# A hybrid S5 and sparse-attention encoder layer: transposing all of x ahead of the modulation, narrower value products, and other shares of stream work

## The chip, the cores and the metric

The kernel runs on one core of one Trainium2 chip. A core has a matrix engine (PE, with its weight loads shown as PEld), a vector engine (DVE), a scalar engine (ACT), a general engine (POOL) and a sync engine (SP) that here mostly issues DMA transfers. The engines run their own instruction queues in order and wait for each other through semaphores. The metric is the device time of one execution in microseconds (us); lower is better.

## What is computed

One layer over 1024 prompt tokens and 32 sample tokens, all treated together as 1056 columns. Cut to what matters here:

```python
mod = silu(c) @ w_mod + b_mod                  # w_mod is 1024 x 3072
shift, scale, gate = split(mod, 3)
h = rms_norm(x, g_norm) * (1 + scale) + shift
z = h @ w_in                                   # u | zs | q | k | v | za | qi | ki | wi | gm
ys = S5 state space model over u, GELU, GLU, SiLU gate zs
score = sum_h wi * relu(qi . ki);  keep the top k keys per query
o = softmax(q . k over kept keys) @ v          # 8 heads of 64, prompt in chunks of 64 (causal)
merged = sigmoid(g_s) * (ys @ w_ps) + sigmoid(g_a) * ((o * silu(za)) @ w_pa)
x_new = x + gate * (merged @ w_o);  y = rms_norm(x_new, g_final)
```

Prompt and sample rows have different c, so different scale and shift. All is float32. The kernel gets its precision by splitting a factor into a high part (fp32r) and a low part, and by three products: high x high, high x low, low x high (`mm3`).

## The kernel before

**Groups of tokens.** The 1056 tokens are cut in three groups of 256, 384 and 416 columns (`BW`, lines 19 and 20; 32 of the last 416 are the sample). Group g has row tiles of 128 tokens (`ROWS`, line 60). h is kept transposed, features on the partitions, in eight slices k of 128 features: `hH` and `hL`, one pair of tiles for each group.

**START.** The order of the beginning is written out by hand in the string `START` (line 48). All engines follow it in program order (a manual schedule is open until line 793). Its tokens, with their digits:
- `sq i`, `ss i`, `sc i`: row tile i of x is squared and summed on ACT (`xsquare`), its reciprocal root made on DVE and POOL (`xrstd`), and scaled on DVE (`xscale`).
- `mm`, `row`, `co`, `ap`: a piece of w_mod is multiplied with the condition vectors on PE (`mod_mm`, L286), copied by ACT (`mod_row`, L291), turned into columns on PE (`mod_cols`, L296), and made into scale and shift by three DVE operations (`mod_apply`). Before, a piece (j, h) is 256 columns of the scale (h = 0) or shift (h = 1) part, loaded in one transfer of 1 MB.
- `xt g k`: PE transposes slice k of group g into PSUM (`xtrans`, L231). `hf g k`: ACT reads that PSUM, applies scale and shift (`xmod`, L237 and L239). `sp g k`: DVE splits the result into hH and hL (`xsplit`, by `split`, L77 and L78).
- `ub q n k`: the three products of slice k of group n with the weights of output block q (0 or 1) of the S5 input u (`ublock`, L271 to L273). `ue`: ACT copies the finished block out.
- `wl q`: the u weights are split. `a n`: n of the small DVE operations that prepare the S5 constants (the list `todo`) are issued. `ld..`: further loads are issued.

Loads are issued by SP in the order of lines 749 to 759 and of the `ld` tokens: three row tiles of x, two pieces of w_mod, the u weights, two more pieces, the second u weights, three more row tiles, and so on, so that x and w_mod arrive mixed. Row tiles lie in borrowed buffers; groups are transposed when their slice of the modulation is known.

**Stream.** The other weight products are jobs of the class `Stream` (`Z`). A job multiplies 128 output features with all three groups: 8 slices x 3 groups x 3 products. `Z.run(us)` issues some microseconds' worth of stream steps on PE at that place of the program, `Z.until(name)` issues steps until a job is done, `Z.upto(name)` says how far the stream may go. So each later stage has PE work between its own steps.

**After START.** `ssm_consts` (line 525) makes S5 constants: four transposes on PE (L529), two copies on ACT, one more transpose (L533), a copy on DVE. Then the loop of line 790 empties `todo` on DVE and asks 2.0 us of stream for each 2.0 us of it. The S5 stage, the glu jobs (their operands ygH and ygL are split on ACT and DVE from the gelu result), the indexer (L1230) and the choice of the keys (L1573, L1575) follow.

**Attention.** Heads are worked in pairs p = 0 to 3. For a pair the loop of line 1720 goes through items: a block of 128 queries (`Rows`), or the sample. For each: scores on PE (L1409), maxima on DVE (L1415), exponentials on ACT (L1422), normalizing, transposes of the probabilities on PE (L1502) and their split into PH and PL (`turn`, L1504 and L1505), and for every second block the value products (`out`, L1519 and L1521) over two blocks of queries, 256 columns, and all their key tiles. The last key tile of such a pair of blocks is not admitted for the first block; `turn` clears its first 128 columns on POOL (L1507, L1508). Each step of the loop asks the stream for `f = FA[p][e] + FF * (i + 1)` us. Pair 3 has the jobs m0 to m7 (products with w_ps) to ask for; behind the loop `Z.until("m7")` issues the rest, and then the products with w_pa begin, first those with the attention result b3 of pair 3.

Of the kernel before, what the change touches and what calls it, by code (L numbers as in the profile page):

```python
# [30 lines left out]
WB = 5  # L31
# [9 lines left out]
KA, LA = 5.0, 1.0  # L41
RE = 2.9
LAG, RS, MS, RM, RB = 4.5, 4.6, 0.008, 14.0, 1
FA, FF, SA, SB = ((1.4, 1.3), (1.45, 1.45), (1.35, 1.35), (1.4, 1.4)), 0.08, 1.0, 2.5
# [19 lines left out]
def body(nc, tc, I, O, dbg=None):  # L64
# [129 lines left out]
    XG, XW = {}, []  # L194

    def xload(i):
        g, r, n = ROWS[i]
        if i < 2:
            xt = stg.tile([128, D], F32, name="xt", tag="stg")
        elif i < 5:  # L200
            xt = XH[i // 4][:, D * (i == 3):D * (i == 3) + D]
        elif i == 5:
            xt = pa.tile([128, D], F32, name="xt", bufs=1)
        else:
            if i % 2 == 0:
# [21 lines left out]
    def xtrans(g, k):  # L227
        px = ps_z("px")
        PX[g, k] = px
        for r, n in enumerate(GROW[g]):  # L230
            te.transpose(px[:, r * 128:r * 128 + n], XG[g][r][:n, k * 128:(k + 1) * 128], idf[:n, :n])  # L231

    def xmod(g, k):
        px = PX.pop((g, k))
        hf = HX[g, k] = pa.tile([128, GM], F32, name="hf", bufs=HF)[:, :BW[g]]
        np_ = min(BW[g], T - B0[g])
        se.activation(hf[:, :np_], px[:, :np_], AF.Identity, bias=sh[:, k, 0:1], scale=scl[:, k, 0:1])  # L237
# [501 lines left out]
    def load(x):  # L739
# [6 lines left out]
        for f in xl:  # L746
            f()
# [1217 lines left out]
```

## Time and profile before

| what | value |
|---|---|
| runs, median of 3 | 998.66 us (997.09 to 1001.67) |
| profiled execution, its time | 997.35 us |
| profiled execution, its span from first to last instruction | 995.6 us |
| mean granted PE clock | 0.991 of full speed |
| DMA in the span | 124.24 MB, mean 125 GB/s |

The profile is of one execution. Its page gives the busy time of each engine and, in 40 slices of the span, the busy share in tenths. Other views of the same trace give stretches of the span (busy us of each engine and the number of its instructions, then the granted clock, the DMA share, GB/s), or a timeline (start in us, duration in us, engine, line, operation, output <- inputs, shapes, how often; in brackets the idle time of the engine before it and what ended that). Durations of matmuls are modelled and overlap; the distance of two starts is what one costs PE. The slices of the other engines and of DMA are:

```profile
DVE  4669979995686868979998977767678786895543
ACT  3642244433555655867999356665676565443211
```

### The profile page before, as it was taken

The numbers are of one execution on the slowest core, as the hardware profiler recorded it, in microseconds if no ns is written. First come the engines' busy times: TensorE is split into PE (matmuls) and PEld (weight loads), VectorE is DVE, ScalarE is ACT, GpSimd is POOL, SyncE is SP. The second block draws the span as 40 slices with busy tenths as digits, with TensorE's granted clock in tenths as the row PEclk, the third lists the DMA queues.
The fourth block names the chain that finished last, engine by engine and source line by source line (L and its number), as shares of the span: only waits on it lengthen the run. The fifth ranks groups of instructions, "written<-read, shape, count | busy, mean of one in ns | idle before, by whom it ended". The sixth has DMA issues, their size and how long they took to land.

```text
span 995.6 us, 16923 instructions
## 1 busy us (share of the span) xinstructions
PE 962.1 (97%) x6034; PEld 898.8 (90%) x6034; DVE 758.3 (76%) x1748; ACT 526.7 (53%) x1127; POOL 229.2 (23%) x435
## 2 busy tenths in 40 slices
PE   4999999999999999999999999999999999999997
PEld 2789999999899899999999999999899988998786
DVE  4669979995686868979998977767678786895543
ACT  3642244433555655867999356665676565443211
POOL 2202400000000003333322852333323222430000
PEclk8899999999999999999999999999999999999999
DMA  9923424536585221424213440231349302662311
GB/s 312 300 66 104 131 70 129 123 94 168 193 255 154 93 64 43 136 80 136 90 65 98 148 145 22 87 120 32 97 132 337 106 23 93 197 211 94 117 64 63
DMA packets 134255, 124.24 MB, mean 125 GB/s; under 512 B 20256, under 2 KB 114932, under 8 KB 134172
## 3 DMA queue, kind: packets, MB, share of 16 engines
q1 hardware_dynamic: 133232, 122.62, 40.0%
q8 instruction: 47, 0.77, 0.3%
q10 hardware_dynamic: 780, 0.52, 0.2%
q14 instruction: 36, 0.29, 0.1%
q0 software_dynamic: 160, 0.03, 0.0%
HBM read 87.74 MB, written 34.83 MB: 123 GB/s over the span
## 4 chain that ended last, share of the span: by engine, by line
PE 54%; DVE 11%; ACT 10%; issue 4%; DMA 1%; POOL 1%; SPq 0%; POOLq 0%; ACTq 0%; DVEq 0%
PE pz L271 9%; PE pz L272 8%; PE pz L273 8%; ACT junkb L1573 7%; PE pss L1409 3%; PE pt L1502 3%; DVE junk L1575 3%; PE psm L1936 3%; PE psm L1934 3%; PE psm L1935 3%; PE pspo L1521 2%; PE pspo L1519 2%; PE pss L1230 2%; PE pss L1231 2%; PE psm L271 1%
## 5 line engine op out<-in xcount | busy, mean ns | idle before, releaser
L271 PE MATMUL pz<-hH,wh 128*128 128x384 f32 (+4 forms) x760 | 258.2, 340 | 0.8 <-ACT zf L1323 0.8
L272 PE MATMUL pz<-hL,wh 128*128 128x384 f32 (+4 forms) x760 | 249.9, 329 | 0.0
L273 PE MATMUL pz<-hH,wl 128*128 128x384 f32 (+4 forms) x760 | 249.8, 329 | 0.0
L264 POOL TENSOR_TENSOR wl<-raw,wh 128x256 fp32r<-128x256 f32 (+1 forms) x176 | 126.4, 747 | 123.6 <-ACT wh L259 119.5
L271 PEld LDWEIGHTS pz<-hH,wh 128*128 128x128 f32 (+1 forms) x760 | 142.5, 188 | 5.9 <-issue 1.7
L272 PEld LDWEIGHTS pz<-hL,wh 128*128 128x128 f32 (+1 forms) x760 | 141.9, 187 | 2.0
L273 PEld LDWEIGHTS pz<-hH,wl 128*128 128x128 f32 (+1 forms) x760 | 141.6, 186 | 1.3
L1573 ACT ACTIVATE junkb<-sco,thr 128x768 bf16<-128x768 f32 (+3 forms) x128 | 96.7, 756 | 29.1 <-DVE thr L1655 18.6
L1575 DVE TENSOR_SCALAR_CACHE_REDUCE junk<-sco,thr 128x1024 bf16<-128x1024 f32 (+2 forms) x96 | 105.4, 1098 | 2.2
L271 PE MATMUL pss<-hH,wh 128*128 128x256 f32 (+2 forms) x288 | 92.8, 322 | 1.5 <-ACT tg L713 1.4
L272 PE MATMUL pss<-hL,wh 128*128 128x256 f32 (+2 forms) x288 | 90.9, 316 | 0.0
L273 PE MATMUL pss<-hH,wl 128*128 128x256 f32 (+2 forms) x288 | 90.6, 315 | 0.0
L263 POOL CAST wh<-raw 128x256 fp32r<-128x256 f32 x84 | 41.2, 529 | 178.3 <-PE pz L272 163.2
L1504 ACT CAST PH<-pt 128x512 fp32r<-128x512 f32 (+2 forms) x96 | 43.0, 482 | 35.2 <-PE pt L1502 32.8
L1505 DVE TENSOR_TENSOR PL<-pt,PH 128x512 fp32r<-128x512 f32 (+2 forms) x96 | 50.4, 552 | 13.1 <-ACT PH L1504 11.9
L1238 DVE SCALAR_TENSOR_TENSOR sco<-rl,wi,sco 128x384 f32<-128x384 f32 (+6 forms) x49 | 45.6, 939 | 18.3 <-ACT rl L1233 17.5
L271 PEld LDWEIGHTS pss<-hH,wh 128*128 128x128 f32 x288 | 55.5, 193 | 3.8 <-POOL wh L263 1.6
L1233 ACT ACTIVATE rl<-pss 128x384 f32<-128x384 f32 (+6 forms) x56 | 41.1, 738 | 28.5 <-PE pss L1231 21.7
L272 PEld LDWEIGHTS pss<-hL,wh 128*128 128x128 f32 x288 | 55.3, 192 | 0.3 <-DVE hL L78 0.2
L273 PEld LDWEIGHTS pss<-hH,wl 128*128 128x128 f32 x288 | 55.2, 192 | 0.0
L1422 ACT ACTIVATE Sm<-Sm,mx 128x128 f32<-128x128 f32 (+8 forms) x68 | 52.7, 774 | 1.3 <-DVE mx L1415 1.3
L1936 PE MATMUL psm<-o,mL 128*128 128x512 f32 (+1 forms) x136 | 52.0, 382 | 0.0
(409 smaller groups left out, 2165.4 us busy)
## 6 DMA issues: line engine op xcount, KB each, us to landing
raw<-in_w_in SPq DMA_DIRECT2D x44, 512.0 KB
thD<-tg SPq DMA_DIRECT2D x16, 528.0 KB
wm<-in_w_mod SPq DMA_DIRECT2D x8, 1024.0 KB
m<-thD SPq DMA_DIRECT2D x8, 528.0 KB
tgl<-thD SPq DMA_DIRECT2D x8, 528.0 KB
rraw<-in_w_mod SPq DMA_DIRECT2D x4, 1024.0 KB
kd<-kd SPq DMA_DIRECT2D x32, 128.0 KB
xo<-in_x_prompt SPq DMA_DIRECT2D x8, 512.0 KB
```

Source lines behind the costliest of these rows:

```text
L263: ge.tensor_copy(wh[:, c], raw[:, c])
L264: leng.tensor_sub(wl[:, c], raw[:, c], f32(wh[:, c]))
L271: te.matmul(ps, wh, xh, start=first, stop=False)
L272: te.matmul(ps, wh, xl, start=False, stop=False)
L273: te.matmul(ps, wl, xh, start=False, stop=last)
L1238: ve.scalar_tensor_tensor(sco[i][:m, :nk], rl[:m, :nk], w, sco[i][:m, :nk], op0=ALU.mult, op1=ALU.add)
L1422: se.activation(P, P, AF.Exp, scale=-1.0, bias=self.mx, accum_out=self.rs)
L1504: se.copy(PH[:, b0:b1_, oc], src)
L1505: ve.tensor_sub(PL[:, b0:b1_, oc], src, f32(PH[:, b0:b1_, oc]))
L1573: se.activation(junkb[:m, :nk], x[:m], AF.Sign, bias=t, accum_out=cnt[:m, k:k + 1])
L1575: ve.tensor_scalar(junk[:m, :nk], x[:m], t, None, op0=ALU.is_lt, op1=ALU.add, accum_out=cnt[:m, k:k + 1])
L1936: te.matmul(ps, ml, wh, start=False, stop=last)
```

## The change

It has four parts.

1. **START.** All nine row tiles of x are loaded first, into the space that hH will take, then half of the u weights (256 columns, four slices), then w_mod in three pieces that hold scale and shift together (256, 256 and 512 features, `MW`), each in parts of 1 MB, and the second half of the u weights before the third piece. Each group of x is transposed as soon as its rows are scaled, two or four slices in one PSUM tile, and copied out of PSUM into tiles `XT` by ACT (`xe`) or DVE (`xd`). When a piece of the modulation is known, its slices are worked for all three groups, one slice after the other. `w n` issues n products that nobody reads. The u products of group 2 get two single PSUM banks. There are 17 of the small DVE operations in START, where there were 36.
2. **ssm_consts** asks 2.0 us of stream between its two sets of transposes.
3. **Value products.** For the last key tile only columns 128 to 255 are multiplied; the clears on POOL go.
4. **Constants.** `FA` asks 0.05 us more for each step in pairs 0 (second head) to 2, and 0.25 less in pair 3; `KA`, the delay between a load of keys and its split, is 4.2 in place of 5.0.

```diff
-WB = 5
+WB = 4
-KA, LA = 5.0, 1.0
+KA, LA = 4.2, 1.0
-FA, FF, SA, SB = ((1.4, 1.3), (1.45, 1.45), (1.35, 1.35), (1.4, 1.4)), 0.08, 1.0, 2.5
+FA, FF, SA, SB = ((1.4, 1.35), (1.5, 1.5), (1.4, 1.4), (1.15, 1.15)), 0.08, 1.0, 2.5
 START = """
-    sq0 ss0 sq1 sc0 ss1 sq2 sc1 ss2 sc2 mm00 srow ldw21 a13 xt00 row00 xt01 co00 mm01 ldw30 row01 wl00 co01
...
+    sq0 ss0 sq1 ss1 sc0 sq2 ss2 sc1 srow xt00 xt04 xd00 sq3 ss3 sc2 xd04 sq4 ss4 sc3 sq5 ss5 sc4 xt10 xt12 xd10
+    sq6 ss6 sc5 xd12 xt14 sq7 ss7 sc6 xt16 xd14 sq8 ss8 sc7 xe16 sc8 xt20 xe20 xt22 xd22 wl00 xt24 xe24 xt26 xd26 wl10
+    mm00 a10 w6 mm01 row0 w3 co0 ap0 w6 hf00 sp00 hf10 sp10 hf20 sp20 ub000 ub100 hf01 sp01 ub010 ub110 hf11 sp11
+    hf21 sp21 ub020 ub120 mm10 a2 ub001 ub101 mm11 row1 ub011 ub111 co1 ap1 ub021 hf02 sp02 hf12 sp12 ub121 hf22 sp22
+    ub002 ub102 hf03 sp03 a1 mm20 ub012 ub112 hf13 sp13 a1 ub022 ub122 mm21 hf23 sp23 ub003 ub103 mm22 wl01 ub013 ub113
+    wl11 mm23 row2 ub023 ldz co2 ap2 hf04 sp04 ub123 hf14 sp14 hf24 sp24 a1 ub004 ub104 hf05 sp05 ub014 ub114 hf15 sp15
...
     def xtrans(g, k):
-        px = ps_z("px")
-        PX[g, k] = px
-        for r, n in enumerate(GROW[g]):
-            te.transpose(px[:, r * 128:r * 128 + n], XG[g][r][:n, k * 128:(k + 1) * 128], idf[:n, :n])
+        px = PX[g, k] = ps_s("px").rearrange("p (j c) -> p j c", j=2 if g else 4)
+        for j in range(px.shape[1]):
+            for r, n in enumerate(GROW[g]):
+                te.transpose(px[:, j, r * 128:r * 128 + n], XG[g][r][:n, (k + j) * 128:(k + j + 1) * 128], idf[:n, :n])
+
+    def xkeep(g, k, copy):
+        px = PX.pop((g, k))
+        for j in range(px.shape[1]):
+            copy(XT[g][k + j], px[:, j, 0:BW[g]])
...
+    def mod_mm(m, i):
+        w = MW[m][1]
+        nk = 1024 // w
+        for k in range(nk):
+            for c in range(2):
+                o = 32 * (2 * (k % 2) + c)
+                te.matmul(pmrow[o:o + 32, 0:w], scP[:, nk * i + k], WM[m, i][:, k, c], start=nk * i + k < 2,
+                          stop=nk * i + k >= 6)
...
     def ssm_consts():
...
             se.mul(dst.rearrange("p k m -> p (k m)"), pt[:, 0:256], sgn_)
+        Z.run(2.0)
...
     def warm(n):
+        if not UP:
+            UP[-1] = ps_z("pw")
         for _ in range(n):
-            te.matmul(pmod[:, 384:512], idf, idf, start=True, stop=True)
+            te.matmul(UP[-1][:, 0:128], idf, idf, start=True, stop=True)
...
+    for i in range(9):
         xload(i)
     uload(0)
+    for m in range(3):
+        if m == 2:
+            uload(1)
+        for i in range(4 if m == 2 else 2):
+            mod_load(m, i)
...
-                if ii == 0:
-                    ge.memset(f32(PH[:, i + 1, oc]), 0.0)
-                    ge.memset(f32(PL[:, i + 1, oc]), 0.0)
...
-                for k in range(nkt):
-                    te.matmul(po[:, 0:256], X.V2[e][:, k], PH[:, k], start=k == 0, stop=False)
-                for k in range(nkt):
-                    te.matmul(po[:, 0:256], X.V2[e][:, k], PL[:, k], start=False, stop=k == nkt - 1)
+                order = [*range(nkt - 2), nkt - 1, nkt - 2]
+                for h, P in ((0, PH), (1, PL)):
+                    for k in order if h or nkt > 2 else order[::-1]:
+                        c0 = 128 * (k == nkt - 1)
+                        te.matmul(po[:, c0:256], X.V2[e][:, k], P[:, k, c0:256], start=not h and k == 0,
+                                  stop=h == 1 and k == nkt - 2)
```

More of the change, by code (lines that the diff above doesn't have):

```diff
@@ L273, in mm3 @@
         te.matmul(ps, wl, xh, start=False, stop=last)
-    sel2 = pa.tile([128, 2], F32, name="sel2", bufs=1)
+    sel4 = pa.tile([128, 4], F32, name="sel4", bufs=1)
     WM, MR_ = {}, {}
-    def mod_load(j, h):
-        wm = WM[j, h] = pa.tile([128, 8, 256], F32, name="wm", tag="wm", bufs=WB)
-        c = (1024, 0)[h] + 256 * j
-        sp.dma_start(wm, w_mod[:, c:c + 256].rearrange("(k p) e -> p k e", p=128))
-    def mod_mm(j, h):
-        for k in range(8):
-            te.matmul(pmrow[32 * (k % 4):32 * (k % 4) + 32, 256 * h:256 * h + 256], scP[:, k], WM[j, h][:, k],
-                      start=k < 4, stop=k >= 4)
@@ L289, in mod_row @@
-    def mod_row(j, h):
-        MR_[j, h] = pa.tile([128, 256], F32, name="mrow", bufs=2)
-        se.copy(MR_[j, h], pmrow[:, 256 * h:256 * h + 256])
-    def mod_cols(j, h):
-        for i in range(2):
-            ch = (8, 0)[h] + 2 * j + i
-            te.matmul(pmod[:, 2 * ch:2 * ch + 2], MR_[j, h][:, 128 * i:128 * i + 128], sel2, start=True, stop=True)
-    def mod_apply(j):
-        kk = slice(2 * j, 2 * j + 2)
-        ks = slice(8 + 2 * j, 10 + 2 * j)
-        bc2 = lambda ap: ap.unsqueeze(2).to_broadcast([128, 2, 2])
-        ve.tensor_tensor(scl[:, kk], pm[:, ks], bc2(bmod[:, ks]), op=ALU.add)
+    MW = ((0, 256), (256, 256), (512, 512))
@@ new lines, in mod_row, with mod_cols, mod_apply @@
+    def mod_row(m):
+        w = MW[m][1]
+        MR_[m] = pa.tile([128, 512], F32, name="mrow", bufs=1)[:, 0:w]
+        se.copy(MR_[m], pmrow[:, 0:w])
+    def mod_cols(m):
+        c0, w = MW[m]
+        for i in range(w // 128):
+            k = c0 // 128 + i
+            te.matmul(pmod[:, 4 * k:4 * k + 4], MR_[m][:, 128 * i:128 * i + 128], sel4, start=True, stop=True)
+    def mod_apply(m):
+        c0, w = MW[m]
+        k0, nk = c0 // 128, w // 128
+        kk = slice(k0, k0 + nk)
+        ks = slice(8 + k0, 8 + k0 + nk)
+        bc2 = lambda ap: ap.unsqueeze(2).to_broadcast([128, nk, 2])
+        ve.tensor_tensor(scl[:, kk], pm[:, kk, 1], bc2(bmod[:, ks]), op=ALU.add)
@@ L724, in body, with uload, uparts @@
     raw = {}
-    def uload(q):
-        raw[q] = wload(w_in[:, C_U + 128 * q:C_U + 128 * q + 128], KT, 128)
-    def uparts(q):
-        UW[q] = wparts(raw[q], KT, 128, leng=ve) if q == 0 else wparts(raw[q], KT, 128, pool=pa, heng=ge, bufs=1)
+    def uload(h):
+        if not h:
+            raw[0] = pa.tile([128, KT, 256], F32, name="uraw", bufs=1)
+        sp.dma_start(raw[0][:, 4 * h:4 * h + 4],
+                     w_in[512 * h:512 * h + 512, C_U:C_U + 256].rearrange("(k p) e -> p k e", p=128))
+    def uparts(q, h):
+        if not h:
+            UW[q] = [(pa if q else wst).tile([128, KT, 128], F32R, name=n, tag=n, bufs=2 - q) for n in ("wh", "wl")]
+        c = slice(4 * h, 4 * h + 4)
+        split(UW[q][0][:, c], UW[q][1][:, c], raw[0][:, c, 128 * q:128 * q + 128], se, ve)
     def srows():
```

103 lines of the change are left out of this document (42 added, 61 removed).

## The prediction

> **What bounds the kernel now.** I read the page first (engine shares, the span in slices), then stretches of the first 50 us with every engine beside the granted clock, then the timelines where PE is not full.
>
> ```profile
> PE 962.1 (97%) x6034; PEld 898.8 (90%) x6034; DVE 758.3 (76%) x1748; ACT 526.7 (53%) x1127; POOL 229.2 (23%) x435
> PE   4999999999999999999999999999999999999997
> ...
> 10.00:20.00 10.00, 6.39 (x57) 4.00 (x61) 6.15 (x24) 2.25 (x4) 1.15 (x2) 0.91 1.11 338
> 20.00:30.00 10.00, 9.90 (x57) 6.70 (x46) 5.27 (x21) 4.83 (x10) 5.06 (x10) 0.50 1.08 359
> 30.00:40.00 10.00, 8.62 (x84) 5.99 (x84) 5.77 (x21) 4.59 (x10) 1.40 (x2) 0.91 1.09 356
> 40.00:50.00 10.00, 10.00 (x83) 9.09 (x82) 7.20 (x22) 8.39 (x16) 0.22 (x2) 1.00 1.00 204
> ```
>
> PE bounds all but the beginning: one slice of 40 is below 9 before the last. A saving counts only if it removes PE work or PE waiting; moving stream work (the weight products that fill gaps) alone changes nothing. The stretches (busy us of PE, PEld, DVE, ACT, POOL, then clock, DMA share, GB/s) show the exception: until about 45 us the DMA engines are full at some 350 GB/s, and from 20 to 30 us PE is busy at half clock.
>
> **START, the part that can gain most.** It ends in before when PE leaves the last u product:
>
> ```profile
> 69.52 0.60 PE L529 MATMUL pt<-idf,cld 128*128 128x128 f32 x4
> 71.10 0.24 PE L533 MATMUL pt<-idf,dl 32*128 32x32 f32 x1 [0.98 <-ACT CR L530]
> 82.81 0.28 PE L271 MATMUL pz<-hH,wh 128*128 128x256 f32 x1
> 94.37 0.28 PE L271 MATMUL pz<-hH,wh 128*128 128x256 f32 x1
> 38.06 1.07 PE L286 MATMUL pmrow<-wm,scP 128*32 128x256 f32 x16
> 22.90 1.94 PE L286 MATMUL pmrow<-wm,scP 128*32 128x256 f32 x16
> 33.34 0.61 PE L296 MATMUL pmod<-sel,mrow 128*128 128x2 f32 x4 [0.50 <-ACT mrow L291]
> 36.97 0.16 DVE L302 TENSOR_TENSOR scl<-pmod,pcol 128x4 f32<-128x4 f32 x1 [3.17 <-PE pmod L296]
> 39.59 0.56 ACT L237 ACTIVATE hf<-px,sh,scl 128x256 f32<-128x256 f32 x1
> ```
>
> The end is at 69.5. One stream job, with the same 72 matmuls as 24 u blocks, takes 94.37 - 82.81 = 11.56 us at full clock, so the 48 u blocks cost 23.1. A 1 MB tile of w_mod costs PE 1.07 at full clock, 1.94 at half; a transpose costs 0.11 (row below), so 0.21 at half. The row copy and its handover stop PE for 0.50; the co products are 0.61 for four records.
>
> After the change nothing can be multiplied before all nine row tiles are squared, scaled, transposed and copied out. What sets that time is DVE, which runs in written order:
>
> ```profile
> 5.22 1.06 ACT L214 ACTIVATE sq<-xt 128x1024 bf16<-128x1024 f32 x1 [1.24 <-DMA xt<-in_x_prompt]
> 6.62 1.06 ACT L214 ACTIVATE sq<-xt 128x1024 bf16<-128x1024 f32 x1 [0.25 <-DMA xt<-in_x_prompt]
> 7.31 0.75 DVE L223 TENSOR_SCALAR xt<-xt,rstd 128x1024 f32<-128x1024 f32 x1 [0.75 <-POOL rstd L219]
> 7.97 0.15 DVE L218 TENSOR_SCALAR ss<-ss 128x1 f32<-128x1 f32 x1
> 8.04 0.20 DVE L167 COPY pcol<-pt 128x48 f32<-128x48 f32 x1
> 246.33 0.28 DVE L1041 COPY sto<-pt 64x128 f32<-64x128 f32 x1 [6.12 <-PE pt L1039]
> 56.10 0.48 ACT L561 COPY uP<-pss 128x384 f32<-128x384 f32 x1 [0.43 <-PE pss L273]
> ```
>
> Row tiles land 1.4 apart (two squares that waited for DMA), so the ninth lands near 16 and is squared by 17. DVE scales a tile in 0.66 (start to next start) and adds 0.15 for ss. Copies out of PSUM grow from 0.20 at 48 columns to 0.28 at 128, 1 ns a column: about 0.36, 0.49 and 0.52 in a run for 256, 384 and 416 columns; DVE has 8, 6 and 4 of these new ones, ACT six of 0.5. Nine scalings (5.9), nine ss (1.4), the first 14 copies (5.8) and srow (0.2) are 13.3. The first scaling, now behind two squares, starts at 7.8: without a wait the last row is scaled at 21; with the waits for transposes that DVE stands behind in its order, at 22.5. Then group 2 goes through two PSUM buffers: 32 transposes and the copies that free the buffers, 3.8 at full clock and about 7 at half. PE reaches mm00 at 26.3 (24.3 without DVE's waits, 30 at half clock). Its data is there: x, half of u and one tile are 5.9 MB, at 0.35 MB a us from 3 us on landed by 20. The start is no longer bound by DMA, but by DVE's copies, which before did not exist (ACT read PSUM directly).
>
> From mm00 to the first u block runs a chain: two tiles 2.1, six warm products between them 1.3 (twelve records, 0.106 each as a transpose), row 0.5, co 0.6, ap 0.7 (three of 0.16 and handovers), hf 0.56 and the split's first half 0.35, together 6.1. From there PE is dense: 48 blocks 23.1, six more tiles 6.4, twelve co records 1.8, and two waits that blocks only partly cover, 0.6 before slice 2 and 1.1 before slice 4. That is 33.0. DVE's splits keep up:
>
> ```profile
> 58.38 0.37 DVE L77 CAST hH<-hf 128x416 fp32r<-128x416 f32 x1
> 58.78 0.59 DVE L78 TENSOR_TENSOR hL<-hf,hH 128x416 fp32r<-128x416 f32 x1
> 59.29 0.37 DVE L77 CAST hH<-hf 128x416 fp32r<-128x416 f32 x1
> ```
>
> 0.92 for the widest group, some 2.5 for three, against 2.9 of PE per slice. The last w_mod tiles reuse buffers freed after mm10 and mm11, near 37 and 39, and so land near 42 and 45; PE wants them at 47 and later. START would end at 26.3 + 6.1 + 33.0 = 65.4; at 69.1 if PE reaches mm00 at 30, a little more if the first products are slow too (69.5); at 63.4 without DVE's waits. I take 66.5, nearer to full clock: **-3.0** (bounds -6.1 and 0, if the clock is back by the first block).
>
> The 2.0 us of stream placed between the two consts transposes covers the 0.98 of PE idle shown above: **-1.0**.
>
> **A debt that START leaves.** It runs 17 of DVE's small constant operations, where it ran 36: 19 of 0.2 are 3.8 us of DVE later, and the loop that empties them asks 3.8 more of stream. With the 2.0 above, 5.8 us of filler is missing later, where the glu jobs wait for the gelu result:
>
> ```profile
> 234.55 0.39 PE L970 MATMUL pss<-HS,G 128*128 128x133 f32 x2
> 250.29 4.38 ACT L75 CAST ygH<-yg 128x1024 fp32r<-128x1024 f32 x4
> 265.22 2.18 DVE L78 TENSOR_TENSOR ygL<-yg,ygH 128x1024 fp32r<-128x1024 f32 x2 [0.99 <-ACT ygH L75]
> 266.38 0.28 PE L271 MATMUL pz<-ygH,wh 128*128 128x256 f32 x1
> ```
>
> PE has 31.7 of other work from 234.7 to 266.4; 25.9 would be left. The chain needs 15.6 to the loaded yg, 8.8 of casts (4.38 for two of four) and 2.2 for the last subtraction, 26.6: **+0.8** (0, if the casts interleave better, to +4, if ACT's evacuations stand in between).
>
> **Half-width value products.** 4 pairs x 2 heads x 4 blocks x 2 parts = 64 matmuls go from 256 to 128 columns.
>
> ```profile
> 648.45 1.19 PE L1519 MATMUL pspo<-PH,V 128*128 128x256 f32 x8
> 649.48 1.10 PE L1521 MATMUL pspo<-PL,V 128*128 128x256 f32 x8
> 645.79 1.09 PE L1502 MATMUL pt<-idf,Sm 128*128 128x128 f32 x8
> 646.64 0.37 PE L1409 MATMUL pss<-kH,qz 128*128 128x256 f32 x1
> 644.38 0.22 PE L1409 MATMUL pss<-kH,qz 128*128 128x128 f32 x1
> 644.43 0.27 PE L1409 MATMUL pss<-kL,qz 128*128 128x128 f32 x1
> 644.55 0.40 PE L271 MATMUL pz<-hH,wh 128*128 128x416 f32 x1
> ```
>
> Eight of 256 columns take 1.03, 0.129 each. Eight transposes of 128 columns, a new weight load each, take 0.85, 0.106: half the columns are not half the time, because the load is then the limit. Two 128-column products between longer ones take 0.17, 0.085 each. So one saves 0.023 to 0.044, or up to 0.07 if its load is always early: 1.5 to 4.5 for 64. The half product stands before a full one, as the last pair of rows does, with loads less far ahead; I take 0.034: **-2.2**. The 64 clears on POOL that go hid behind PE; nothing for them.
>
> **Stream shares, KA.** Pair 3 runs some 20 steps and asks 0.25 less in each, 5.0 us; pairs 0 to 2 ask 0.05 more in 9 to 17, 2.1. So 2.9 of m7 moves behind the loop, where PE waits today:
>
> ```profile
> 841.75 0.35 PE L273 MATMUL pz<-b,wl 128*128 128x416 f32 x1
> 843.26 0.75 PE L271 MATMUL psm<-b3H,wh 128*128 128x256 f32 x3 [1.15 <-ACT b3H L75]
> 766.00:842.00 76.00, 74.60 (x507) 70.04 (x505) 57.72 (x165) 43.33 (x99) 17.78 (x45) 1.00 0.24 72
> ```
>
> It can cover 1.15, if ACT's cast of b3 isn't itself queued behind a weight cast that waits for m7: **-0.8** (0 to -1.8, with two shorter gaps behind it). In pair 3 PE idles 1.4 of 76 and DVE is busy 76%; with 7% less filler the softmax chain of DVE and ACT shows more often: **+0.8** (0 to +4). KA moves a load by under a microsecond inside that: nothing.
>
> **Sum.** -3.0 - 1.0 + 0.8 - 2.2 - 0.8 + 0.8 = -5.4 on the profiled execution's 997.35 (its span 995.6 and 1.8 around it): 991.95. The median of the three runs shown is 1.3 above the profiled one, so 993.3.
>
> **Rivals.**
> *Slow clock to mm00.* PE was granted 0.50 from 20 to 30 us although it was busy 9.90 of 10, and the new beginning is transposes with pauses between them. Then START ends at 69.5, as today, and -2.4 is left: 996.3. For it: that row. Against it: the 0.91 before and after, and the warm products. The Trainium skill ("TensorE: Matmul & The Clock Gate", Part 4: PE-mode transpose) says that transposes do not count as a busy PE in the way products do; by that this rival holds. The row agrees in part only: the half clock also lay over u products.
> *Slow clock in the slices, the slower case.* If the half clock holds for some 14 us from the first block on (it held from before 20 to past 30 here), blocks at 11.56 / 24 = 0.48 become 0.87, and each such us loses 0.45: 6.1. START ends near 75.6, the whole is +3.7: 1002.4. It decides against the change from 5.4 us of half clock on, and two such stretches give 1008. Against it: PE is then dense, and the clock was 1.00 from 40 on.
> *Pair 3 starves.* The softmax chain keeps its period and the 5.0 less stays idle: +4 in place of +0.8, and START as forecast: 996.5.
> *Everything hides.* START ends at 63.4, value products save 0.07, no debt, the end -1.8: -6.1 - 1.0 - 4.5 - 1.8 + 0.8 = -12.6: 986.1.
>
> **How the numbers follow.** My forecast 0.37, slow clock to mm00 0.22, slow slices 0.11, pair 3 starving 0.10, everything hiding 0.20. About 5 us, 0.5%, is what a measurement can tell here. The forecast lies on that edge, with two thirds of its chance beyond it (0.25), the last rival wholly (0.20), of the others 0.05: faster 0.50. Slower by over 0.5% is the slow slices that last longer than one stretch or meet another loss: 0.09. The range goes from 985 to 1001: it leaves out the slow slices and little else.
>
> **What would show it.** The start of L529 in the consts: near 66.5, and mm00 near 26 to 27; DVE full from 8 to 25 us; the granted clock from 20 to 40 us; no gap of 0.98 before L533; the gap at the first glu product; mean spacing of value products; the gap before the first b3 product, and PE's idle time in pair 3. I am wrong if DVE's copies are much faster or slower than 1 ns a column, or the clock is half behind 30 us.

## The result, and the profile after

The changed kernel takes 1011.07 us (median of 4 runs, 1007.25 to 1013.32) against 998.01 for the kernel before: ratio 1.012, 95% interval 1.0078 to 1.0162. It is slower, by some 13 us, or 1.2%; the forecast was 993.3 in a range of 985 to 1001. The profiled run of the changed kernel took 1007.25 with a span of 1005.5, so between the two profiles 9.9 us are to be explained.

The page of the changed kernel, the lines that stood first in the prediction:

```profile
PE 965.6 (96%) x6016; PEld 899.2 (89%) x6016; DVE 763.8 (76%) x1765; ACT 528.8 (53%) x1131; POOL 210.2 (21%) x363
PE   4999999999899999999999999999999999999997
```

PE is busy 3.5 us longer although it has less to compute, and the span grew by 9.9: some matmuls ran more slowly, and PE waited more. Walking through both traces by the same landmarks (PE's idle time added up between them) gives the places:

| stretch | before | after | difference | forecast |
|---|---|---|---|---|
| end of START (first S5 constants transpose) | 69.5 | 75.6 | +6.1 | -3.0 |
| PE idle in the constants | 1.0 | 0.4 | -0.6 | -1.0 |
| PE idle in the S5 stage | 1.9 | 3.4 | +1.5 | 0 |
| PE idle at the first qi0 product | 0 | 3.3 | +3.3 | +0.8 (placed at the first glu product) |
| PE idle from glu to the pairs | 3.3 | 2.3 | -1.0 | 0 |
| PE idle in the pairs | 3.7 | 4.8 | +1.1 | +0.8 |
| PE idle behind the last value product | 1.9 | 1.2 | -0.7 | -0.8 |
| 320 value products, start to next start | 40.7 | 40.4 | -0.3 | -2.2 |

They add up to +9.4 of the 9.9. Two places hold nearly all of it: START, and the stretch from the S5 stage to qi0.

**START.** Stretches of the changed kernel (busy us of PE, PEld, DVE, ACT, POOL, then granted clock, DMA share, GB/s), then PE's timeline and DVE's:

```profile
20.00:30.00 10.00, 7.38 (x33) 4.84 (x31) 5.93 (x13) 2.29 (x5) 4.35 (x5) 0.67 1.04 332
30.00:40.00 10.00, 10.00 (x77) 6.70 (x76) 4.93 (x19) 2.08 (x5) 0.15 (x2) 0.74 0.34 111
...
18.10:21.50 3.40, 3.40 (x16) 2.99 (x16) 2.40 (x6) 0.00 (x0) 0.99 (x1) 0.50 1.09 348
21.50:25.00 3.50, 1.82 (x11) 0.98 (x9) 3.06 (x8) 0.86 (x2) 2.43 (x3) 0.99 1.09 348
25.00:28.40 3.40, 2.46 (x10) 1.61 (x11) 0.88 (x1) 1.04 (x3) 0.93 (x2) 0.50 1.09 349
28.40:31.80 3.40, 3.40 (x13) 2.21 (x14) 1.69 (x3) 0.54 (x2) 0.00 (x0) 0.50 0.37 118
31.80:35.20 3.40, 3.40 (x24) 1.70 (x23) 1.40 (x3) 1.28 (x3) 0.15 (x2) 0.50 0.02 5
35.20:38.60 3.40, 3.40 (x38) 2.49 (x34) 1.94 (x11) 0.37 (x1) 0.00 (x0) 1.00 0.55 154
```

```profile
10.51 3.62 PE L223 MATMUL pss<-idf,xr 128*128 128x128 f32 x16
...
18.02 3.72 PE L223 MATMUL pss<-idf,xr 128*128 128x128 f32 x16 [0.87 <-DVE xr L215]
...
25.94 0.31 PE L223 MATMUL pss<-idf,xt 32*128 32x32 f32 x1 [1.41 <-DVE xt L215]
...
33.69 1.78 PE L291 MATMUL pmrow<-wm,scP 128*32 128x256 f32 x16
...
40.80 0.36 PE L268 MATMUL pss<-hH,wh 128*128 128x256 f32 x1
...
75.58 0.60 PE L538 MATMUL pt<-idf,cld 128*128 128x128 f32 x4
```

```profile
19.11 1.02 DVE L228 COPY xT<-pss 128x384 f32<-128x384 f32 x2 [1.15 <-PE pss L223]
23.41 0.73 DVE L215 TENSOR_SCALAR xr<-xr,rstd 128x1024 f32<-128x1024 f32 x1
24.58 1.30 DVE L215 TENSOR_SCALAR xt<-xt,rstd 32x1024 f32<-32x1024 f32 x1 [0.44 <-POOL rstd L211]
```

The first product with w_mod starts at 33.7, not at 26.3. DVE scales the last row (the 32 sample rows, whose tile lies in a staging buffer) only at 24.6 to 25.9, 3.4 later than reckoned, after standing at copies that waited for PE (1.15 in the first row) and because the sample rows take 1.30 where a full tile takes 0.73. Then the 32 transposes of group 2 take 7.75 (25.94 to 33.69) in place of 3.8: the clock is at half until 35.2. From there to the first u block it is 7.1 (forecast 6.1), and from there to the end 34.8 (33.0).

The 1.30 isn't the price of 32 partitions. In each of the 18 traces exactly one scaling takes 1.30, and it is the one that starts some 0.1 behind a clear of 0.83 on POOL. In the kernel before that scaling is a full tile of 128 partitions (first two rows; the 32 sample rows take 0.74 there), in the changed kernel the clear meets the sample rows (third row):

```profile
10.31 0.83 POOL L537 MEMSET zrow<- 16x896 f32 x1
10.40 1.30 DVE L223 TENSOR_SCALAR xh<-xh,rstd 128x1024 f32<-128x1024 f32 x1 [0.66 <-POOL rstd L219]
...
24.50 0.83 POOL L547 MEMSET zrow<- 16x896 f32 x1
```

No run moved the clear, so that it holds the scaling up is likely and not shown.

The clock column needs a caution. Its record begins with the first change of the clock, at 14.7 here, and counts as whole what lies before. The distances of the transposes tell more: the sixteen from 10.51 on take 3.62, like the sixteen from 18.02 on that ran at 0.50, so PE was at half until 14.7 too. In all 18 traces equal matmuls are 0.21 us apart ahead of the first record, where they are 0.11 apart at whole clock.

**From the S5 stage to qi0.** ACT's and then PE's timeline in the changed kernel:

```profile
259.23 0.37 ACT L1084 COPY zki<-pz 72x256 f32<-72x256 f32 x1 [3.90 <-DMA out_sim_p<-sto]
264.20 4.28 ACT L73 CAST ygH<-yg 128x1024 fp32r<-128x1024 f32 x4 [4.60 <-DMA yg<-yD]
268.38 0.48 ACT L1084 COPY zki<-pz 72x384 f32<-72x384 f32 x1
```

```profile
268.91 0.45 PE L268 MATMUL pz<-hH,wh 128*128 128x384 f32 x1 [3.27 <-ACT zki L1084]
```

ACT's second copy of the ki job stands in the written order behind casts of the gelu result, and these wait for a transfer that landed at 264.2. PE had finished its part of ki at 265.6 and waits for the PSUM buffer of that copy. In the kernel before, the same casts started at 250.29, early enough. The S5 stage is thus 14.0 late (last gelu operation on DVE 252.96 against 238.94), the stream jobs only 7.8 (first ki product 253.88 against 246.05). Counting the stream products on PE between the end of START and the first S5 product gives 381 before and 417 after: 36 more at 0.16 us are 5.8 us of filler spent early. That is the 3.8 of DVE's small operations and the 2.0 of the consts: with the new START alone the stream stands 24 products ahead, with the consts line alone 12.

### The profile page after: what moved, and what is told of

It is laid out like the page before. It is cut to its first block, busy times and chain, and to the rows that moved or that the text cites. A ratio compares the mean times of both kernels' runs of the same rounds, so it can differ in the third digit from the quotient of the medians.

```text
span 1005.5 us, 16804 instructions
## 1 busy us (share of the span) xinstructions
PE 965.6 (96%) x6016; PEld 899.2 (89%) x6016; DVE 763.8 (76%) x1765; ACT 528.8 (53%) x1131; POOL 210.2 (21%) x363
## 4 chain that ended last, share of the span: by engine, by line
PE 64%; DVE 16%; ACT 12%; issue 4%; DMA 3%; POOL 0%; SPq 0%; POOLq 0%; ACTq 0%; DVEq 0%
PE pz L268 10%; PE pz L270 10%; PE pz L269 10%; ACT junkb L1583 7%; PE pspo L1530 3%; PE pss L1420 3%; PE pt L1513 3%; DVE junk L1585 3%; PE psm L1946 3%; PE psm L1944 3%; PE psm L1945 3%; PE pss L1241 2%; PE pss L1242 2%; PE psm L268 1%; PE psm L269 1%
## 5 line engine op out<-in xcount | busy, mean ns | idle before, releaser
L261 POOL TENSOR_TENSOR wl<-raw,wh 128x256 fp32r<-128x256 f32 (+1 forms) x172 | 117.1, 710 | 139.3 <-ACT wh L256 136.7
L268 PE MATMUL pss<-hH,wh 128*128 128x256 f32 (+1 forms) x272 | 85.1, 313 | 1.8 <-DVE hH L75 1.2
L269 PE MATMUL pss<-hL,wh 128*128 128x256 f32 (+1 forms) x272 | 84.4, 310 | 0.2
L270 PE MATMUL pss<-hH,wl 128*128 128x256 f32 (+1 forms) x272 | 83.9, 309 | 0.0
L268 PEld LDWEIGHTS pss<-hH,wh 128*128 128x128 f32 x272 | 51.5, 189 | 6.5 <-DVE hH L75 1.9
L269 PEld LDWEIGHTS pss<-hL,wh 128*128 128x128 f32 x272 | 51.0, 188 | 0.9 <-DVE hL L76 0.8
L1944 PE MATMUL psm<-o,mH 128*128 128x512 f32 (+1 forms) x136 | 51.7, 381 | 0.0
```

The source lines that it names most:

```text
L261: leng.tensor_sub(wl[:, c], raw[:, c], f32(wh[:, c]))
L268: te.matmul(ps, wh, xh, start=first, stop=False)
L269: te.matmul(ps, wh, xl, start=False, stop=False)
L270: te.matmul(ps, wl, xh, start=False, stop=last)
L1944: te.matmul(ps, mh, wh, start=first, stop=False)
```

## Experiments

All ratios are against the kernel before, timed beside each kernel on the same chip.

### Which part loses: START alone, and the rest alone

The first kernel has the new START and everything else as before, the second the old START and everything else new:

```diff
 # START alone: taken back from the change
-KA, LA = 4.2, 1.0
+KA, LA = 5.0, 1.0
-FA, FF, SA, SB = ((1.4, 1.35), (1.5, 1.5), (1.4, 1.4), (1.15, 1.15)), 0.08, 1.0, 2.5
+FA, FF, SA, SB = ((1.4, 1.3), (1.45, 1.45), (1.35, 1.35), (1.4, 1.4)), 0.08, 1.0, 2.5
-        Z.run(2.0)
 # and the value products of full width, with the clears on POOL
```

> Only the new START; value products, the shares of pair 3, the key delay and the extra 2.0 us of stream are as before. Theory A (the whole loss comes from START: its own end 6.1 us later, and 3.3 us more at the glu hand-over because the S5 stage trails the stream): the first S5 constants transpose starts at 75.6, the gap of 0.98 in the consts is back, the wait of the first qi0 product is 1 to 3.5 us (2.0 us less filler was used up), total 1006 to 1012. Rival B (the other parts lose as much as START): 1001 to 1004.

> The old START with the three other parts: half-width value products, 2.0 us of stream in the consts, the new shares and the key delay. Theory A: START ends at 69.5 as before, consts gap gone (-1.0), value products -0.3 (a half product takes 60 ns where a full one took 120, but the full one behind it takes 171), tail and pair 3 cancel: 996 to 998 against 998. Rival B: these parts lose, 1000 to 1004. My blind terms would give -3.2: 995.

START alone: 1013.11, ratio 1.0145 (1.0124 to 1.0167). The rest alone: 1001.72, 1.0037 (1.0021 to 1.0052). START holds the loss, as theory A has it (a little over its range), but the rest isn't neutral: 3.4 us are lost there too, which is rival B's number for that kernel. In its trace START ends at 69.3 as before, but the first glu product comes 3.4 late (269.8 against 266.4). The two losses, 14.8 and 3.4, add up to more than the 13.1 of the whole change, so the parts act on each other. The other signs of theory A came for START alone: it ends at 75.4, the gap in the consts is back (1.00) and PE waits 1.40 at qi0. But its trace also has half-clock stretches behind waits at 243.3 and 765.6, which the profile of the changed kernel doesn't have.

### The 2.0 us of stream in the consts

Which of the parts is it? One kernel has this line alone, one has it and gives the 2.0 us back ahead of the S5 stage:

```diff
 # both
+        Z.run(2.0)
 # the second besides
-FS = (17, 2.5, 1, 1, 2.5, 7, 2.5, 0.6)
+FS = (15, 2.5, 1, 1, 2.5, 7, 2.5, 0.6)
```

> The kernel before with only the 2.0 us of stream put between the two sets of transposes of the consts. My blind term: the gap of 0.98 goes, 997.4. Theory F (2.0 us less stream is left for the S5 stage and every weight split of a stream job falls elsewhere among DVE's S5 steps; the last S5 products then wait 2 to 4 us, and a half-clock stretch of 3.4 us follows that wait): 1000 to 1002, with S5's last product near 240 in place of 234.7.

> The kernel before with the 2.0 us of stream in the consts, and 2.0 us less asked before the first block of the S5 stage (15 in place of 17), so that from there on the stream stands where it stood. Theory F (the 2.0 us cost 3.9 because a weight split of the stream then falls on DVE ahead of an S5 step while ACT has not yet cast its high part): S5 ends near 234, no wait at the last S5 products, the gap of 0.98 stays covered: 997.4. Rival I (the loss comes from the consts themselves or from the shorter debt to glu): 1000 to 1002 again.

Alone: 1002.36, ratio 1.0038 (1.0023 to 1.0054). Given back: 997.35, 0.9993 (0.9983 to 1.0003). So one line that covers a wait of 0.98 costs 3.9 us, and moving the same amount of stream back undoes all of it. Theory F holds. How it works is seen in the S5 stage, first on DVE in the kernel before:

```profile
214.48 0.69 DVE L864 TENSOR_TENSOR G<-G,e 128x512 f32<-128x512 f32 x1
215.09 1.26 DVE L978 SCALAR_TENSOR_TENSOR a<-a,Yq 128x1064 f32<-128x1064 f32 x1
...
220.38 1.22 DVE L264 TENSOR_TENSOR wl<-raw,wh 128x1024 fp32r<-128x1024 f32 x1
```

then on DVE, ACT and PE with the 2.0 us in the consts:

```profile
215.39 0.69 DVE L865 TENSOR_TENSOR G<-G,e 128x512 f32<-128x512 f32 x1
218.84 1.23 DVE L264 TENSOR_TENSOR wl<-raw,wh 128x1024 fp32r<-128x1024 f32 x1 [2.75 <-ACT wh L259]
219.98 1.26 DVE L979 SCALAR_TENSOR_TENSOR a<-a,Yq 128x1064 f32<-128x1064 f32 x1
```

```profile
217.35 0.52 ACT L714 ACTIVATE tg<-pz 128x416 f32<-128x416 f32 x1 [1.89 <-PE pz L273]
217.77 1.04 ACT L259 CAST wh<-raw 128x1024 fp32r<-128x1024 f32 x1
```

```profile
230.98 0.47 PE L970 MATMUL pss<-Uq,Tq 128*128 128x133 f32 x2 [1.40 <-DMA Tq<-kD]
233.79 0.81 PE L971 MATMUL pss<-HS,G 128*128 128x133 f32 x2 [2.35 <-DVE HS L953]
```

Before, the weight split wl of the next stream job stood behind the gelu step `a` in DVE's order, at 220.4, and its high part was ready. Now the stream is four steps ahead (393 products against 381), so the split stands ahead of `a`: it waits 2.75 for ACT, which itself waits for PE to finish a group of the stream job, and with its own 1.2 it delays the S5 chain by 4.0 (`a` goes from 215.09 to 219.98, the DVE step ahead of it only from 214.48 to 215.39). PE meets this some 15 us later and waits 1.40 and 2.35; from 232.0, between the two waits, to 238.9 it runs at half clock (0.83 on average from 220 to 240).

### Half-width value products, and the shares

> The kernel before with only the half-width value products (and without the clears on POOL that they make needless). Theory G (the weight load sets the pace: the half product takes 60 ns, but the full one behind it 171 in place of 120): 64 products save 0.3 us, total within 0.5 of 998.4. My blind term: 2.2 less, 996.2. Rival: these products cost the 3.4 us that the kernel without the new START lost: 1001.7.

> The kernel before with the new shares of stream work in the pairs and the new key delay alone. My blind terms were -0.8 at the tail and +0.8 in pair 3; the two traces show the waits behind the last value product 1.77 to 1.03 us, and PE idle in pair 3 1.85 to 2.54: 998.4, within 0.5. Rival: the shares lose 2 or more: 1000.4.

```diff
 # the first kernel, on the kernel before
-                for k in range(nkt):
-                    te.matmul(po[:, 0:256], X.V2[e][:, k], PH[:, k], start=k == 0, stop=False)
...
+                        c0 = 128 * (k == nkt - 1)
+                        te.matmul(po[:, c0:256], X.V2[e][:, k], P[:, k, c0:256], start=not h and k == 0,
+                                  stop=h == 1 and k == nkt - 2)
 # the second, on the kernel before
-KA, LA = 5.0, 1.0
+KA, LA = 4.2, 1.0
-FA, FF, SA, SB = ((1.4, 1.3), (1.45, 1.45), (1.35, 1.35), (1.4, 1.4)), 0.08, 1.0, 2.5
+FA, FF, SA, SB = ((1.4, 1.35), (1.5, 1.5), (1.4, 1.4), (1.15, 1.15)), 0.08, 1.0, 2.5
```

The products: 996.97, ratio 0.9985 (0.9975 to 0.9995), so 1.5 us faster within 0.5 to 2.5. The shares: 996.86 against 997.23, ratio 0.9997 (0.9988 to 1.0005), nothing that can be told. The same pair of blocks whose rows stand in the prediction, now in the changed kernel:

```profile
658.72 1.18 PE L1530 MATMUL pspo<-PH,V 128*128 128x256 f32 x8
659.74 1.10 PE L1530 MATMUL pspo<-PL,V 128*128 128x256 f32 x8
660.68 0.35 PE L268 MATMUL pz<-hH,wh 128*128 128x416 f32 x1
```

Eight products, one of them of half width, take 1.02 to the next start, where eight full ones took 1.03. Over all 64 of them the median distance from a half product to the next is 60 ns, where a full one takes 120; but from the full product behind it to the next start it is 171. Together 231 against 240, which is 0.6 us over the 64. PE's weight loads start 0.11 to 0.12 us apart all through these rows, so what the half product gives up, the full one behind it waits. The trace of the first kernel gives 40.2 us for the 320 products (40.7 before), and 420.1 us from the wait near 575 to the end (421.0 before), 0.9 less. The interval of the timing holds 0.9 and also the 2.2 of the prediction, while the 0.3 expected lies just outside it. Put on another kernel (further down) the same edit takes the ratio from 0.9989 to 0.9983, 0.6 us, which the intervals don't separate from nothing.

### The clock in START

> The changed kernel with 31 unread 128-column products put between the transposes of START at the places where PE waited, from 14 to 26 us. Theory D (the clock is halved because PE pauses between 14.7 and 26): no half clock behind about 25 us, group 2's 32 transposes take 3.9 in place of 7.75, the first w_mod product starts near 30 and START ends near 71.5, total 4 us below the changed kernel. Rival E (the half clock is a fixed amount, 13.65 us in both profiles, whatever PE does): the half stretch only shifts, START ends at 75 to 77.

> The kernel before with 16 unread products ahead of its first w_mod product and 12 ahead of its third, where PE waited 3.9 and 1.9 us. Theory D (pauses of PE bring the half clock): the half-clock stretch from 18.2 to 31.8 goes; START ends only some 0.8 earlier, near 68.7, because PE then waits for w_mod near 34: 997.5. Rival E (a fixed amount of half clock): no change of the clock or only a shift, 998.4.

```diff
 # the changed kernel, in xtrans, ahead of the transposes of row tile r
+                if not j:
+                    warm({(1, 0, 0): 4, (1, 0, 1): 8, (1, 0, 2): 4, (1, 4, 0): 2, (1, 6, 0): 3, (2, 0, 0): 2, (2, 0, 2): 2, (2, 0, 3): 6}.get((g, k, r), 0))
 # the kernel before, in START
-    ... sc2 mm00 srow ... co01 ap0 mm10 ...
+    ... sc2 w16 mm00 srow ... co01 w12 ap0 mm10 ...
```

The changed kernel with these products: 1005.36, ratio 1.007 (1.0046 to 1.0094), 5.7 less than the changed kernel's median (4 expected). Its stretches:

```profile
10.00:20.00 10.00, 9.58 (x67) 9.04 (x68) 6.89 (x20) 6.12 (x12) 3.34 (x5) 1.00 1.07 348
20.00:30.00 10.00, 9.46 (x69) 7.53 (x67) 6.67 (x13) 3.27 (x8) 4.17 (x5) 1.00 1.03 328
30.00:40.00 10.00, 9.85 (x87) 7.80 (x85) 7.39 (x26) 4.92 (x10) 0.15 (x2) 1.00 0.63 213
```

The clock is whole from 13.5 to the end of START, the first w_mod product starts at 30.2 and START ends at 71.4: theory D, nearly to the tenth, but for group 2, which takes 4.75 at whole clock and not 3.9. The half clock is no fixed amount. The other traces say the same: in the five kernels that have the new START without these products, PE is at half until 34.9 to 36.0 but for one or two stretches of 3.4; in the four with them the clock becomes whole between 13.5 and 16.8 and stays so in START, but for one stretch in one of them (e14, at 57.0).

In the kernel before the same products give 997.68, ratio 0.9989 (0.9978 to 1.0001). Its clock is then whole from 12.1 on, with one half stretch left (from 29.2 to 32.6), but START ends at 69.3, because w_mod is then what PE waits for. The old START without them bears this out: in five more traces PE is at half until 25.7 to 33.1, and START ends at 69.3 to 71.0. The later ends go with half stretches behind some 31 us: with one at 34.7 or 35.9 START ends at 71.0 or 70.5, and in the kernel with all gains (further down), which has these products and yet three such stretches from 30.8 to 41.0, at 72.1.

### DVE's order in START

Two kernels build on the one with unread products: the copies of group 1 out of PSUM go to ACT behind its last square, and then the unread products behind row 4 are left out:

```diff
-xt10 xt12 xd10 sq6 ss6 sc5 xd12 xt14 sq7 ss7 sc6 xt16 xd14 sq8 ss8 sc7 xe16 sc8 xt20
+xt10 xt12 sq6 ss6 sc5 sq7 ss7 sc6 sq8 ss8 sc7 sc8 xe10 xt14 xe12 xt16 xe14 xe16 xt20
 # the second besides
-warm({(1, 0, 0): 4, (1, 0, 1): 8, (1, 0, 2): 4, (1, 4, 0): 2, (1, 6, 0): 3, (2, 0, 0): 2, (2, 0, 2): 2, (2, 0, 3): 6}.get((g, k, r), 0))
+warm({(1, 0, 0): 4, (1, 0, 1): 8, (1, 0, 2): 4}.get((g, k, r), 0))
```

> The kernel with unread products between the transposes, and besides three of DVE's copies out of PSUM (group 1) moved to ACT, behind its last square; DVE then scales all rows without standing behind a transpose. Theory A (DVE's order sets the last scaling, at 25.9, and so the first w_mod product): last scaling ends near 22, first w_mod product near 26.5, START ends near 67.7, total 3.7 below the kernel with unread products alone (1005.4): 1001.7. Rival H (group 2 waits for PSUM buffers or for ACT's copies instead): first w_mod product at 29 to 30, total 1004 to 1005.

> The kernel with unread products and copies of group 1 on ACT, without the 15 unread products behind row 4 (in the run with them the last row was scaled at 23.1, but they held PE until 25.6). Theory A: group 2 is transposed from 23.4 on in 4.7 us, first w_mod product near 28.2, START ends near 69.4, total 1002.8, if the clock stays whole. Rival: the clock falls to half once PE pauses there, first w_mod product at 30 or later, 1005 or more.

The first: 1005.07, ratio 1.0061 (1.0042 to 1.0079), no gain. The last row was scaled at 23.1, but the unread products, now the longest queue, kept PE from its transposes until 25.6: a miss of the experiment's own making. The second: 1001.41, ratio 1.0031 (1.002 to 1.0042). Its PE timeline:

```profile
22.42 0.24 PE L225 MATMUL pss<-idf,xt 32*128 32x32 f32 x1 [0.60 <-DVE xt L215]
...
27.16 1.07 PE L293 MATMUL pmrow<-wm,scP 128*32 128x256 f32 x16
```

With DVE free and the clock whole, group 2 takes 4.74 and the first w_mod product starts at 27.2; START ends at 68.3, 1.2 before the old one. That is what the new order is worth in START at its best; in the trace of a further kernel with the same START (e14 below) a half-clock stretch at 57.0 moves its end to 70.2, 0.7 behind the old one. And this kernel is still 3 us slower than the one before.

### The stream used up early

> The changed kernel with 37 of the small DVE constant operations in START in place of 17, spread where DVE idles. If the S5 stage trails the stream by 6.2 us because 20 of these operations were left for later (theory A), the S5 products start near +7 instead of +12 us against before, the wait of 3.3 us at the first qi0 product goes, and the total is 3 us below the changed kernel, START's end unmoved at 75.6. Rival C (these operations are slow wherever they stand and delay the splits in START): START ends 2 to 4 later and nothing is won.

> The changed kernel with the casts of the gelu result written 4.0 us of stream later, and 4.0 less asked behind them, so that ACT copies two groups of the ki job out before it stands at casts that wait for a transfer. Theory J (the 3.3 us at the first qi0 product are an order on ACT, not missing PE work): that wait falls below 0.5 and the glu products start 1 to 3 us earlier: 1008 to 1010 against 1011. Rival K (PE lacks work, so the wait moves to the first glu product): total as the changed kernel, 1011.

> The changed kernel with 5.8 us less stream asked ahead of the first S5 block (11.2 in place of 17): the trace of the changed kernel shows 417 stream products between the end of START and the first S5 product where the kernel before shows 381, 36 more, at 0.16 us each. Theory L (beside START's end, 6.1 later, the loss is these 5.8 us of stream used up early): first S5 product near 137.6, last near 242, the wait of 3.3 at the first qi0 product gone, total 5 us below the changed kernel: 1006. Rival M (DVE's S5 constants are the bound, so PE only waits for them): 1009 to 1011.

> The same 5.8 us taken back in the changed kernel whose START runs at whole clock (unread products up to row 4, copies of group 1 on ACT; START ended at 68.3, total 1001.4). Theory L: first S5 product near 130.4, last near 234, no wait at qi0, total 996 to 998, so the new START is then worth about 1 us. Rival M: DVE idled only 5.6 us in that stretch, PE waits for the S5 constants instead: 999 to 1001.

```diff
 # e3: a10 a2 a1 a1 a1 a1 a1 in START become
+    a16 a5 a2 a2 a3 a3 a4
 # e10
-YR = 3.9, 2.0, 2.0, 8.0, 3.0
+YR = 7.9, 2.0, 2.0, 4.0, 3.0
 # e13 on the changed kernel, e14 on the one whose START ends at 68.3
-FS = (17, 2.5, 1, 1, 2.5, 7, 2.5, 0.6)
+FS = (11.2, 2.5, 1, 1, 2.5, 7, 2.5, 0.6)
```

More small operations in START (e3; the edit makes them 35, not the 37 of the expectation): 1009.68, ratio 1.0111 (1.009 to 1.0132). The stream stands 24 products ahead in place of 36, and the wait at qi0 falls from 3.27 to 0.64; but the wait before the last S5 products grows from 0.88 to 1.89 with a half-clock stretch behind it. Partly as expected, and mostly given back.

Later casts (e10): 1009.24, ratio 1.0112 (1.0093 to 1.0131). ACT and PE:

```profile
261.88 0.47 ACT L1084 COPY zki<-pz 72x384 f32<-72x384 f32 x1 [1.64 <-PE pz L270]
265.69 4.43 ACT L73 CAST ygH<-yg 128x1024 fp32r<-128x1024 f32 x4 [3.34 <-DMA yg<-yD]
```

```profile
276.64 0.36 PE L268 MATMUL pz<-ygH,wh 128*128 128x256 f32 x1 [1.26 <-DVE qis L1080]
```

The copy now stands ahead of the casts and the wait at qi0 is gone; 1.26 and two of 0.55 appear at the glu products. Against the end of START the first glu product comes 1.8 earlier (200.4 behind it in place of 202.1). That is theory J, for about half of the wait: the other half has moved, as rival K says, because PE has nothing else to do.

The stream given back (e13): 1008.01, ratio 1.0105 (1.0087 to 1.0124). Up to the glu products theory L is right to the tenth: 384 products stand before the first S5 product (417), that product starts at 137.4 (expected 137.6), the S5 stage idles 1.8, there is no wait at qi0, and ACT's casts start at 255.0 (264.2):

```profile
254.99 4.40 ACT L73 CAST ygH<-yg 128x1024 fp32r<-128x1024 f32 x4
259.28 0.49 ACT L1084 COPY zki<-pz 72x384 f32<-72x384 f32 x1
```

The first glu product comes at 272.0 in place of 277.7. But of these 5.7 us only 0.4 are left at the end of the profile, and the ratio is 0.15% better, not the 0.5% expected: PE idles 2.3 more between glu and the pairs and 2.5 more in the pairs, where waits of 1.47 at a value product and 1.44 before a transpose stand out. The same happens on the faster START (e14): 999.96, ratio 1.0024 (1.0016 to 1.0033), with the first glu product at 266.7, level with the kernel before, and then 2.4 lost behind it, with the same waits. That the jobs of the pairs too were set to where the stream stood would explain it; no run tests that.

### The gains together

> The kernel before with 28 unread products in START and with half-width value products: the two parts that gained alone (0.7 and 1.5). If they add: 996.2; if the first was chance: 997.

> The kernel before with what gained alone: 28 unread products in START, half-width value products, and 2.0 us of stream in the consts taken back ahead of the S5 stage. If the three add (0.7 + 1.5 + 1.0): 995.2. If they share one cause: 996.5.

Unread products and half-width products on the kernel before: 996.57, ratio 0.9983 (0.9973 to 0.9993). With the 2.0 us in the consts and 15 in place of 17 as well: 995.29 against 997.23, ratio 0.9979 (0.9967 to 0.9991). That beats both kernels; the last step from the one to the other is inside the intervals. That 995.29 meets the 995.2 of the expectation is luck: this was reckoned from 998.4, and the kernel before took 997.23 here. The gain is 1.9 to 2.1 where the three parts add up to 3.2, and the interval (0.9 to 3.3) holds both readings.

## Why the prediction was wrong

**START, -3.0, measured +6.1: the step that failed first.** "PE reaches mm00 at 26.3 (24.3 without DVE's waits, 30 at half clock)" put the last scaling at 22.5 and took whole clock for granted. The last scaling ended at 25.9, and group 2 took 7.75. The first of these is mostly DVE's order: with the clock whole from 13.5 on the last scaling still ended at 25.4, and with three copies moved to ACT besides at 23.1, or 22.4 with fewer unread products. In it the sample rows took 1.30, reckoned at 0.66. The second is mostly the clock: at whole clock group 2 took 4.74, where the text had 3.8. The bound of 30 had the half clock for group 2 but not DVE's lateness, so the true 33.7 lay outside it. Removing both in experiments brought 27.2, near the forecast. The stretch behind it was short by 2.8 in all (7.1 and 34.8 for 6.1 and 33.0): the first w_mod tile still at half clock (1.78), and small losses each time PE goes between blocks and w_mod tiles.

The rival "slow clock to mm00" named the mechanism, and the row that spoke for it (0.50 at PE busy 9.90) was in the text. I let two weak reasons outweigh it: the clock before and after, and warm products that stand only behind the transposes. The first was also misread: the 0.91 from 10 to 20 counts as whole what lies ahead of the first record, and a w_mod tile at 11.19 took 1.94 there, like the one at 22.90. The rival "slow clock in the slices" did name 75.6 for the end of START, but by luck: the half clock lay ahead of the first block (40.8), not from it on. Two signs named beforehand tell the failure: DVE, which was to be full from 8 to 25 us, was busy 5.93 of 10 from 20 to 30, and the clock was at half behind 30.

**Consts, -1.0, measured +3.9 when made alone.** The wait of 0.98 did go. "Moving stream work alone changes nothing" was the false step: a stream step carries a weight split for ACT and DVE, whose place among the S5 steps counts for more than the idle time covered.

**Debt, +0.8, measured +3.3 at qi0 and +1.5 in the S5 stage.** The amount was right (5.8 us; 36 products show it; its own sum, 26.6 less 25.9, gives 0.7), and "if ACT's evacuations stand in between" was the mechanism of the 3.3 and lay in its range. The sum took the low end, at the glu products, and had no term for the S5 stage.

**Value products, -2.2 (1.5 to 4.5), timed -1.5 (0.5 to 2.5), in the traces -0.3 to -0.9.** The timing alone doesn't refute the size; the spacing of the products does. "Two 128-column products between longer ones take 0.17" was the wrong row: it doesn't count what the next product pays. The row of eight transposes at 0.106 each, a new weight load each, was the nearer one, and even it was kind: 0.023 for each product where the spacing leaves 0.009.

**Tail and pair 3, -0.8 and +0.8: about right.** Behind the last value product PE idles 1.2 in place of 1.9, the wait for b3 is gone, and pair 3 idles 2.4 in place of the 1.4 that the prediction's row shows:

```profile
857.38 0.75 PE L268 MATMUL psm<-b,wh 128*128 128x256 f32 x3 [1.03 <-ACT b L73]
```

Alone, these shares and KA gave no difference that can be told, as summed.

**The range** ended at 1001 because each rival was priced alone, with the debt at its low end. Slow clock to mm00 with the debt at +4 would have been 999.5 by the text's own numbers, and with the true 33.7 some 1003. What stays open is why the median lies 13 above the kernel before where the profiles lie 9.9 apart; the three other runs of the changed kernel weren't profiled. The recorded mean clocks of the four fall as the times rise (0.991, 0.990, 0.987, 0.985), which suggests further half-clock stretches like those of START alone; where they lay isn't on record.

## What to carry to other kernels

Work on PE that is split off to start early should be looked at for the clock: transposes with pauses between them can run at half speed, and a few unread products in the pauses bring the clock back, free as long as they end before the data is there. A filler that is moved between stages is not free even where PE is full: ask which operations on other engines it brings along and whose queue they now stand ahead of. A matmul of half width saves half only if the weight loads behind it can come faster too. And where the record of the clock hasn't begun, the distance of equal matmuls tells it.

## What the runs showed of the hardware

Half clock came in stretches of 3.41 us or two, three or four times that (but for the one that a trace may begin or end in), also late in the kernel, behind a wait. PE's busy time in the stretch before, in it and behind it, in the kernel with unread products, then two such stretches of the changed kernel around its wait of 3.27:

```profile
262.70:266.10 3.40, 1.00 (x6) 1.00 (x7) 3.37 (x3) 3.40 (x4) 0.00 (x0) 1.00 1.03 421
266.10:269.50 3.40, 3.40 (x12) 3.40 (x11) 3.12 (x5) 2.00 (x4) 0.00 (x0) 0.50 1.07 358
269.50:272.90 3.40, 3.40 (x20) 3.39 (x20) 0.99 (x3) 1.65 (x3) 0.00 (x0) 1.00 0.44 111
```

```profile
263.90:267.30 3.40, 1.74 (x10) 1.01 (x8) 1.01 (x1) 3.10 (x3) 0.00 (x0) 1.00 1.01 413
267.30:270.70 3.40, 1.79 (x10) 1.79 (x11) 3.28 (x4) 3.40 (x4) 0.00 (x0) 1.00 1.03 420
```

In the first kernel the wait falls into one stretch, PE is busy 1.00 of 3.40 there, and the next stretch runs at half: 12 matmuls in place of 20, a loss of about 1.7 us on top of the wait. In the changed kernel a wait about as long lies across two stretches, busy 1.74 and 1.79, and nothing follows. The Trainium skill ("TensorE: Matmul & The Clock Gate", Part 1: The HAM clock gate) gives a free-running window of 3413 ns, and the clock throttles there after an idle one. The trace agrees with that length; but a window busy 29% was enough here. Busy share alone doesn't decide it: two windows busy 51% and 53% were not enough here, yet the half clock of the kernel before at 18.2 followed a stretch just as busy (1.74 of 3.40) with transposes and w_mod products, and that of e14 at 57.0 followed one busy 2.54 of 3.41.

What brings the clock back isn't settled. In the changed kernel the stretch from 18.1 to 21.5 held transposes alone and the next ran at whole clock; the one from 28.4 to 31.8 did too and the next ran at half. In the kernel before PE was busy for 3.40 of 3.40 with u products and the next stretch was still at half:

```profile
25.00:28.40 3.40, 3.40 (x16) 3.25 (x16) 1.76 (x7) 2.38 (x6) 3.16 (x6) 0.50 1.04 368
28.40:31.80 3.40, 3.30 (x17) 2.76 (x20) 2.87 (x9) 2.20 (x5) 1.61 (x4) 0.50 1.09 349
```

A scaling of 1024 elements took 1.30 us on DVE where it began just behind a clear on POOL, with 128 partitions as with 32, and 0.73 to 0.76 otherwise, in all 18 traces.
